# A two-layer hybrid decoder trunk on one core: attention in visits of two token tiles, retention's queries and keys in one product, weight places and delays set anew

## The chip, the core and the metric

The kernel runs on one NeuronCore of a Trainium2 chip. A core has a matrix engine (TensorE, PE in the profile, with its weight loads as PEld), a vector engine (VectorE, DVE), a scalar engine (ScalarE, ACT), GpSimd (POOL) and a SyncE queue (SP) that issues most DMAs. Each engine works through its own list of instructions in order and waits on semaphores for the others. The metric is the device time of one execution in microseconds, lower is better. Before the change three runs took 1002.16, 1005.88 and 1008.02 us, the median being 1005.88.

## What is computed

Two layers (DEPTH = 2) over 1024 tokens of width 1024, all in 32-bit floats. In each layer one projection feeds three groups of heads whose outputs are gated, joined and projected back:

```python
h = rms_norm(x, pre_gain) * (1.0 + scale) + shift
proj = h @ w_in
(aq, ak, av, ag, rq, rk, rv, rg, gq, gk, gv, gg, ga) = jnp.split(proj, IN_SPLITS, axis=-1)
a_out = sliding_window_attention(aq, ak, av, sinks) * jax.nn.silu(ag)
r = retention(rq, rk, rv.reshape(B, S, RET_HEADS, RET_DV))
r_out = rms_norm(r).reshape(B, S, RET_W) * jax.nn.silu(rg)
g_out = rms_norm(g, gla_norm_gain).reshape(B, S, GLA_W) * jax.nn.silu(gg)
y = jnp.concatenate([a_out, r_out, g_out], axis=-1) @ w_out
return x + gate * rms_norm(y, post_gain)
```

`scale`, `shift` and `gate` come from a product with `w_mod`; `g` is gated linear attention (GLA); `aq`, `ak`, `rq` and `rk` are rotated by position first. Attention has 8 query heads on 2 key heads, a window of 128 tokens and a learned sink per head in the softmax. Retention has 4 heads of 64 with a fixed decay per head and runs in chunks of 128.

## The kernel before

**Tiles.** The tokens make 8 tiles of 128 (t = 0 to 7), two to a pair (p), four to a half (hf). The input weights are loaded in units of 256 columns: gg, rg (gates), rq, rk, rv (retention), gqk, gv (GLA), kv, aq0, aq1 (attention), ag0, ag1 (its gates), and o0 to o3 of the output projection. For accuracy each operand of the large products is held as a rounded part and a remainder; a product sums three of the four combinations (`PASSES`) over 8 blocks of depth, so 24 matmuls (`accum`). `project` makes one tile by one unit, so matmuls of 256 columns; `project_T` makes 128 weight columns by four tiles, matmuls of 512 columns, its two halves named by `both`. All matmuls are recorded on one line, that of the helper `mult` (L173), and transposes on that of `transp` (L188); products go into `mm` banks of PSUM (3), everything else into `aux` banks (5).

**Stages of a layer.** Gates (`do_gates`), retention (the loop over p with rq, rk, rv), GLA's products (`do_gqk`, `do_gv`) with keys and values of attention (`do_kv`), rotated queries (`attn_rot`), attention with the ag products, output projection. Retention, GLA and attention cores are generators (`ret_core`, `gla_core`, `attn_q`), called jobs, cut into steps by `yield`.

**What sets the order.** TensorE's order is the order in which the program is written. While it is built, `clk` adds up the assumed TensorE time; every `yield` names a delay from the table `L`, and `pump`, called between and inside products, runs each job step that is due. So the table decides how many products lie between, say, a tile's scores and its transposes. `flag` and `await_flag` make steps wait for one another on the same clock. In a product with 512 columns `pump` is called after every 4 matmuls, with 256 after every 7. The other engines' lists are ordered by a scheduler from the same program.

**Attention before.** `attn_run` visits one tile of one half and one key head g: `attn_q` makes the scores of 4 heads in two `aux` banks (12 matmuls, 64 rows of the array each), moves them to SBUF (`smx`, line 157 for the previous block's copy on ScalarE, line 936 for the masked one on VectorE), takes the maximum (938), four exponentials (941), the reciprocal (944) and the scaling on POOL (945). After `aq3` it transposes the four heads into one bank; ScalarE copies, POOL masks (`affine_select`). After `aq4` it multiplies with the values `va` and their differences `vd`, and stores the result to `aoS`.

**Weights.** A unit arrives in four parts of 256 KB through staging buffers (`st`, 5, shared with the `w_mod` stream), each issued on SP; ScalarE or VectorE writes the rounded part (157, 159), VectorE or POOL the remainder (546). `PLACE` says into which of the seven places of SBUF a unit goes, and so which earlier unit must be done with. `load` is called when that one is.

Of the kernel before, what the change touches and what calls it, by code (L numbers as in the profile page):

```python
# [10 lines left out]
F32 = mybir.dt.float32  # L11
# [36 lines left out]
TURNED = ("gqk", "aq0", "aq1", "ag0", "ag1")  # L48
TOKEN_AT, PLAIN_AT, TURNED_AT, OUT_AT, BLOCK_AT = 48, 0, 48, 0, 64
PLAIN = 2  # L50
SW = dict(W00=6, T1=3, W11=4, W10=5, T2=2, T3=0, T4=1)
TOK = ((1, 2, 3, 4), (3, 4, 0, 1))
PLACE = []
for _t, _w in zip(TOK, (0, 2)):
    PLACE.append(dict(gg=_w, rg=5, rq=6, rk=_w, rv=5, gqk=6, gv=_w, kv=5, aq0=6, aq1=_w, ag0=5, ag1=_w,
                      o0=_t[0], o1=_t[1], o2=5, o3=6))
# [37 lines left out]
def trunk(ctx: ExitStack, tc: tile.TileContext, ins, cst, out):  # L94
# [53 lines left out]
    def both(x, y):  # L148

        return bass.AP(x.tensor, x.offset, [x.ap[0], (y.offset - x.offset, 2), (1, 256)])  # L150
# [489 lines left out]

    def project_T(pm, l, hf, w, c):
# [259 lines left out]
    def attn_run(l):  # L901

        for hf in range(2):
            for g in range(2):
                for t in range(4 * hf, 4 * hf + 4):
                    yield (lat("aq7" if hf else "aq1", l), ("q", l, hf, g))
                    yield (0.0, ("kT", l, t))
                    job(attn_q(l, t, g, kv[(hf, g)]))

    def attn_q(l, t, g, q):  # L910

        sm = gp.tile([P, 4, 129], F32, tag="smx", name=nm("smx"), bufs=SMB)
        V.tensor_copy(sm[:, :, 128], sink8[:, l, 4 * g:4 * g + 4])
        if t == 0:
            G.memset(sm[:, :, 0:128], -1e30)
        else:
            vd = gp.tile([P, P], F32, tag="vd", name=nm("vd"), bufs=3)
            G.tensor_tensor(vd, kv["v"][t], kv["v"][t - 1], ALU.subtract)
        pss = [aux(), aux()]
        n = P if t == 0 else 2 * P  # L920
        cols = slice((t + 1) * P - n, (t + 1) * P)
        for j in range(2):
            qc = slice(P * (t % 4), P * (t % 4) + P)
            for i, (a, b) in enumerate(PASSES):
                for r in range(2):
                    rr = slice(64 * r, 64 * r + 64)
                    mult(pss[r][:, j * n:(j + 1) * n], q[rr, a, j, qc], kv["kT"][b][rr, cols],
                         i == 0, i == 2, n / 4600.0)
        if t % 4 == 3:
            flag(("s", l, t // 4, g))  # L930
        for r in range(2):
            pv = pss[r][:, 0:2 * n].rearrange("p (j c n) -> p j c n", j=2, n=P)
            sv = sm[:, r:4:2, 0:128]
# [794 lines left out]
```

## Time and profile before

| | |
|---|---|
| three runs | 1002.16, 1005.88, 1008.02 us |
| profiled execution | 1000.26 us |
| its span, first to last instruction | 998.5 us |
| mean granted TensorE clock | 0.987 |
| TensorE idle over 1 us, by its waits | 29.2 us in fifteen groups, the largest 7.4 us |
| DMA moved | 148.76 MB, 149 GB/s on average |

The lines of the profile name engine, line, operation and tiles as out<-in; times are us from the start of the span. A timeline row gives start, length, engine, instruction, count and, in brackets, the idle time before it with what released it. Because matmuls are pipelined and their ends are modelled, a row's length overlaps the next one; what a group costs TensorE is the distance from its start to the next start.

### The profile page before, as it was taken

The numbers are of one execution on the slowest core, as the hardware profiler recorded it, in microseconds if no ns is written. First come the engines' busy times: TensorE is split into PE (matmuls) and PEld (weight loads), VectorE is DVE, ScalarE is ACT, GpSimd is POOL, SyncE is SP. The second block draws the span as 40 slices with busy tenths as digits, with TensorE's granted clock in tenths as the row PEclk, the third lists the DMA queues.
The fourth block names the chain that finished last, engine by engine and source line by source line (L and its number), as shares of the span: only waits on it lengthen the run. The fifth ranks groups of instructions, "written<-read, shape, count | busy, mean of one in ns | idle before, by whom it ended". The sixth has DMA issues, their size and how long they took to land.

```text
span 998.5 us, 19629 instructions
## 1 busy us (share of the span) xinstructions
PE 961.3 (96%) x7133; PEld 825.5 (83%) x7133; DVE 690.5 (69%) x1698; ACT 409.6 (41%) x1152; POOL 236.0 (24%) x275
## 2 busy tenths in 40 slices
PE   5798999999999999999999999999999999999896
PEld 2598999888998777778889999998899877777675
DVE  3779856857767778664588285685666577676886
ACT  2476411324332556542356242123333267664231
POOL 2210101232330234330113010113332034555000
PEclk8899999999999999999999999999999999999998
DMA  9832613523326255668646151343132433487883
GB/s 315 296 114 79 186 48 88 161 89 101 110 81 188 79 154 155 203 192 259 228 150 203 49 175 38 106 136 116 41 107 85 127 90 123 131 247 242 262 268 136
DMA packets 129968, 148.76 MB, mean 149 GB/s; under 512 B 14112, under 2 KB 94284, under 8 KB 129872
## 3 DMA queue, kind: packets, MB, share of 16 engines
q1 hardware_dynamic: 124176, 137.96, 45.2%
q10 hardware_dynamic: 5696, 9.56, 2.5%
q8 instruction: 56, 0.92, 0.4%
q14 instruction: 40, 0.33, 0.1%
HBM read 109.20 MB, written 36.18 MB: 146 GB/s over the span
## 4 chain that ended last, share of the span: by engine, by line
PE 75%; DVE 10%; DMA 7%; ACT 3%; issue 3%; POOL 2%; SPq 1%; ACTq 0%; POOLq 0%; DVEq 0%
PE mm L173 56%; PE aux L173 14%; PE aux L188 4%; DMA st<-in_w_in_dram 2%; POOL sm L650 2%; DMA t<-mixF 1%; DMA xk<-in_x_dram 1%; DMA t<-in_x_dram 1%; DMA aoS<-t 1%; DMA a<-mixS 1%; DVE arena L546 1%; DVE arena L723 1%; ACT t L666 1%; DVE t L715 1%; SPq L162 1%
## 5 line engine op out<-in xcount | busy, mean ns | idle before, releaser
L173 PE MATMUL mm<-arena 128*128 128x256 f32 (+2 forms) x1824 | 299.5, 318 | 4.2 <-DVE t L1008 2.7
L173 PE MATMUL mm<-arena,arena 128*128 128x256 f32 (+2 forms) x1824 | 297.4, 316 | 0.3 <-DVE t L1008 0.3
L173 PEld LDWEIGHTS mm<-arena 128*128 128x128 f32 x1824 | 255.3, 191 | 28.4 <-issue 3.3
L173 PEld LDWEIGHTS mm<-arena,arena 128*128 128x128 f32 x1824 | 252.5, 188 | 23.9 <-issue 4.3
L650 POOL TENSOR_TENSOR sm<-sm,mhalf 128x1 f32<-128x1 f32 (+1 forms) x64 | 55.9, 874 | 347.3 <-DVE sm L649 334.9
L173 PE MATMUL mm<-arena,mx 128*128 128x512 f32 (+1 forms) x564 | 128.2, 383 | 1.4 <-ACT kept L1355 1.4
L173 PEld LDWEIGHTS mm<-arena,mx 128*128 128x128 f32 x564 | 101.6, 188 | 22.9 <-ACT kept L1355 1.8
L157 ACT ACTIVATE t<-aux 128x256 f32<-128x256 f32 (+2 forms) x124 | 55.9, 468 | 73.7 <-PE aux L188 62.5
L157 ACT ACTIVATE arena<-st 128x512 fp32r<-128x512 f32 x94 | 55.9, 626 | 51.2 <-PE mm L173 19.0
L546 POOL TENSOR_TENSOR arena<-st,arena 128x512 fp32r<-128x512 f32 x31 | 43.3, 1401 | 133.2 <-ACT arena L157 96.7
L945 POOL TENSOR_TENSOR smx<-smx,sm 128x512 f32<-128x512 f32 x32 | 36.4, 1138 | 124.2 <-DVE sm L944 114.2
L546 DVE TENSOR_TENSOR arena<-st,arena 128x512 fp32r<-128x512 f32 x77 | 59.1, 787 | 5.9 <-ACT arena L157 3.7
L941 ACT ACTIVATE smx<-smx,sm 128x129 f32<-128x129 f32 x128 | 49.9, 392 | 27.8 <-DVE sm L938 27.8
L188 PE MATMUL aux<-c_ident,t 128*128 128x128 f32 (+1 forms) x292 | 48.6, 284 | 7.8 <-DVE t L681 7.4
L375 DVE SCALAR_TENSOR_TENSOR acc<-st,c_act,acc 128x512 f32<-128x512 f32 x60 | 45.4, 757 | 14.1 <-DMA st<-in_w_mod_dram 13.6
L188 PEld LDWEIGHTS aux<-c_ident,t 128*128 128x128 f32 (+1 forms) x292 | 35.2, 145 | 15.0 <-DVE t L681 9.4
L989 ACT ACTIVATE t<-aux 128x256 f32<-128x256 f32 x32 | 12.3, 384 | 75.7 <-PE aux L173 72.2
L173 PEld LDWEIGHTS aux<-t,mx 32*128 32x128 f32 (+1 forms) x896 | 39.5, 187 | 3.8 <-issue 2.0
L713 ACT ACTIVATE t<-aux,mod,mod 128x128 f32<-128x128 f32 x68 | 25.7, 459 | 37.0 <-DVE t L1262 19.4
L173 PE MATMUL aux<-t,mx 32*128 32x32 f32 (+1 forms) x896 | 40.6, 272 | 0.0
L936 DVE COPY_PREDICATED smx<-c_curmask,aux 128x256 f32<-128x256 int32 x64 | 25.5, 447 | 16.0 <-ACT smx L157 13.0
L1262 DVE SCALAR_TENSOR_TENSOR t<-t,sm,t 128x512 f32<-128x512 f32 x32 | 24.0, 780 | 17.8 <-DMA t<-in_x_dram 11.5
(223 smaller groups left out, 1382.9 us busy)
## 6 DMA issues: line engine op xcount, KB each, us to landing
st<-in_w_in_dram SPq DMA_DIRECT2D x96, 256.0 KB, 3.1
st<-in_w_mod_dram SPq DMA_DIRECT2D x64, 256.0 KB, 2.8
st<-in_w_out_dram SPq DMA_DIRECT2D x52, 256.0 KB, 3.7
mx<-mixS SPq DMA_DIRECT2D x20, 512.0 KB, 4.9
mixS<-t SPq DMA_DIRECT2D x72, 128.0 KB, 3.1
wm<-in_w_mod_dram SPq DMA_DIRECT2D x12, 512.0 KB, 6.6
t<-in_x_dram SPq DMA_DIRECT2D x24, 256.0 KB, 4.9
t<-tabS SPq DMA_DIRECT2D x16, 256.0 KB, 3.8
```

What stands on the lines that cost most here:

```text
L157: A.activation(dst, src, AF.Copy)
L173: T.matmul(dst, lhsT, rhs, start=start, stop=stop)
L188: T.transpose(dst, src, idn)
L375: V.scalar_tensor_tensor(acc, wt, c_act[:, k:k + 1], acc, ALU.mult, ALU.add)
L546: e.tensor_tensor(lo, st, f(hi), ALU.subtract)
L650: G.tensor_tensor(r, r, mhalf[:, :w], ALU.pow)
L713: A.activation(hf[:, ks], at[kt], AF.Identity, scale=gain, bias=shift)
L936: V.copy_predicated(sv, curmask.unsqueeze(1).to_broadcast((P, 2, P)), pv[:, :, n // P - 1, :])
L941: A.activation(sm[:, h, :], sm[:, h, :], AF.Exp, bias=mx[:, h:h + 1], accum_out=sums[:, h:h + 1])
L945: eng("pn").tensor_tensor(sm[:, :, 0:128], sm[:, :, 0:128], rs.unsqueeze(2).to_broadcast((P, 4, P)), ALU.mult)
L989: A.activation(sq, po, AF.Square)
L1262: V.scalar_tensor_tensor(xt[j], yg[j], r, xt[j], ALU.mult, ALU.add)
```

## The change

Five things change together.

1. `attn_q` becomes `attn_two`: a visit takes the tiles t and t + 1. Scores of both (four `aux` banks), then softmax of both, one delay, transposes of both (two banks), one delay, value products of both into the two halves of one bank, one copy of 512 columns, two stores. There are 16 visits in place of 32. `smx` has 4 buffers in place of 3, `vd` 4 in place of 3, the small tiles 13 in place of 11.
2. In retention `project2` multiplies a tile with rq and rk in one product of 512 columns; `both` joins the two units, for which they stand in the same arena. For each pair the values (rv) come first, then the joint product of either tile. `rv` is loaded after gg, `rk` after rg.
3. `PLACE` and `SW` are dealt anew, `rq` and `rk` start at a different offset of their place, and o3, ag1 and W00 are loaded at exchanged points.
4. The table `L` is set anew: `aq1` 6.0 to 12.0, `aq3` 10.21 to 14.0, `rc1` 0.8 to 8.5, `ld2` 1.2 to 0.8, and some forty more.
5. Two paddings of SBUF and a DMA scratch size (4096 to 1024) differ.

```diff
-TURNED = ("gqk", "aq0", "aq1", "ag0", "ag1")
+TURNED = ("gqk", "aq0", "aq1", "ag0", "ag1", "rq", "rk")
...
-    PLACE.append(dict(gg=_w, rg=5, rq=6, rk=_w, rv=5, gqk=6, gv=_w, kv=5, aq0=6, aq1=_w, ag0=5, ag1=_w,
-                      o0=_t[0], o1=_t[1], o2=5, o3=6))
+    PLACE.append(dict(gg=_w, rg=5, rq=6, rk=5, rv=_w, gqk=_w, gv=5, kv=6, aq0=_w, aq1=5, ag0=6, ag1=_w,
+                      o0=_t[0], o1=_t[1], o2=6, o3=5))
...
+    def project2(l, t, u, v):
+        w0, w1 = used(l, u), used(l, v)
+        await_flag(("hT", l, t))
+        c = slice((t % 2) * P, (t % 2) * P + P)
+        h = hT[(l, t // 2)]
+        pm = mm()
+        accum(pm.rearrange("p (s n) -> p s n", s=2), lambda a, k: h[:, a, k, c],
+              lambda b, k: both(w0[:, b, k, 0:256], w1[:, b, k, 0:256]))
+        return pm
...
-    def attn_q(l, t, g, q):
+    def attn_two(l, ts, g, q):
...
+        for t in ts:
+            pss[t] = [aux(), aux()]
...
+                for i, (a, b) in enumerate(PASSES):
+                    for r in range(2):
+                        rr = slice(64 * r, 64 * r + 64)
+                        mult(pss[t][r][:, j * n:(j + 1) * n], q[rr, a, j, qc], kv["kT"][b][rr, cols],
+                             i == 0, i == 2, n / 4600.0)
...
+        yield lat("aq3", l)
+
+        mv = {}
+        for t in ts:
+            pp = aux()
+            for h in range(4):
+                transp(pp[:, h * P:(h + 1) * P], sms[t][:, h, 0:128], ident)
+            pf = t2()
+            copy("pf0", pf, pp)
...
         yield lat("aq4", l)
         po = aux()
...
-        ao = t1()
-        copy("aoc", ao, po[:, 0:256])
...
+        ao = t2()
+        copy("aoc", ao, po)
+        for i, t in enumerate(ts):
+            dma("sao", aoS[t, :, 2 * g:2 * g + 2, :], ao[:, 256 * i:256 * i + 256].rearrange("p (k q) -> p k q", k=2))
+            flag(("ao", l, t, g), lat("aq5", l))
...
-            for name in ("rq", "rk", "rv"):
...
+            for t in (2 * p, 2 * p + 1):
+                pm = project2(l, t, "rq", "rk")
+                q, k = (ret_rot(t, pm[:, 256 * i:256 * i + 256], d) for i, d in enumerate((qdec, kdec)))
+                job(ret_core(l, t, q, k, rr[t]))
+                pump()
+            if last:
+                load(l, "gv")
+                load(l, "kv")
...
-B2, B1, BS, BST, MMB, SMB = 10, 8, 11, 5, 3, 3
+B2, B1, BS, BST, MMB, SMB = 10, 8, 13, 5, 3, 4
```

How this moves instructions is seen in the built order of each engine. First TensorE in layer 0's attention, before the change: one visit's value products, a stretch of products, the next visit's transposes, and the first rows of another visit's scores (ten more rows alternate between the same two banks).

```order
L173 MATMUL aux_4965<-t_847_4837,va_3446 64x256 x2
L173 MATMUL aux_4965<-t_848_4839,vd_4672 64x256 x2
L173 MATMUL mm_4923<-arena_322 128x512 x20
L188 MATMUL aux_5004<-c_ident,smx_4860 128x128 x4
L173 MATMUL aux_5021<-kT_3225,mx_4358 128x256
L173 MATMUL aux_5022<-kT_3225,mx_4358 128x256
```

The same place of TensorE's order after the change (`smx` is a tile's softmax, `va` and `vd` its values, `mm` the product stream, `kT` and `mx` keys and queries).

```order
L174 MATMUL mm_4618<-arena_72 128x512 x12
L189 MATMUL aux_4720<-c_ident,smx_4471 128x128 x4
L189 MATMUL aux_4729<-c_ident,smx_4475 128x128 x4
L174 MATMUL mm_4618<-arena_72 128x512 x8
L174 MATMUL mm_4752<-arena_322 128x512 x24
L174 MATMUL mm_4789<-arena_322 128x512 x4
L174 MATMUL aux_4794<-t_853_4725,va_3249 64x256 x2
L174 MATMUL aux_4794<-t_854_4727,vd_4473 64x256 x2
L174 MATMUL aux_4794<-t_856_4734,va_3411 64x256 x2
L174 MATMUL aux_4794<-t_857_4736,vd_4477 64x256 x2
L174 MATMUL aux_4819<-kT_3030,mx_4183 128x256
L174 MATMUL aux_4820<-kT_3030,mx_4183 128x256
```

Small matmuls now come in groups twice as long with longer stretches of products between: 36 products lie between a pair's transposes and its value products.

A little later in TensorE's order after the change, the last two rows of that visit's 24 score matmuls and what follows them.

```order
L174 MATMUL aux_4833<-kT_3031,mx_4183 128x256
L174 MATMUL aux_4834<-kT_3031,mx_4183 128x256
L189 MATMUL aux_4878<-c_ident,smx_4641 128x128 x4
L189 MATMUL aux_4887<-c_ident,smx_4645 128x128 x4
L174 MATMUL mm_4789<-arena_322 128x512 x20
L174 MATMUL mm_4935<-arena_322,arena_72 128x512 x16
L174 MATMUL aux_4974<-t_886_4883,va_3558 64x256 x2
```

Here the transposes of the previous visit follow the scores with no product between; their second bank, the fifth `aux` bank after the first of these scores, is that score bank again.

Then ScalarE at the end of layer 0's retention, before the change. The rows from `st` are conversions of the last three parts of kv that ScalarE takes, `t_419` is the copy of a tile's turned queries and keys for which `ret_core` waits, `t_410` a tile's values, `t_415` a finished output.

```order
L157 ACTIVATE arena_322<-st_2483 128x512
L157 ACTIVATE arena_322<-st_2495 128x512
L157 ACTIVATE t_410_2428<-mm_2367 128x256
L157 ACTIVATE arena_322<-st_2524 128x512
L157 ACTIVATE t_415_2443<-aux_2440 128x256
L157 ACTIVATE t_419_2458<-aux_2453 128x512
```

The same place on ScalarE after the change; `t_400` is now the copy that `ret_core` waits for.

```order
L158 ACTIVATE arena_322<-st_2262 128x512
L1015 ACTIVATE t_383_2166<-aux_2151 128x256
L158 ACTIVATE arena_322<-st_2303 128x512
L158 ACTIVATE t_389_2186<-aux_2183 128x256
L158 ACTIVATE arena_322<-st_2349 128x512
L158 ACTIVATE arena_322<-st_2367 128x512
L158 ACTIVATE t_400_2229<-aux_2224 128x512
```

`st_2262` is the last part of gv; the two last parts of kv stand directly ahead of the copy, where before one part and a finished output did.

## What was predicted

> **What bounds the kernel now.** I read the page's busy line first, then the chain that ended last, then TensorE's waits, then the windows.
>
> ```profile
> PE 961.3 (96%) x7133; PEld 825.5 (83%) x7133; DVE 690.5 (69%) x1698; ACT 409.6 (41%) x1152; POOL 236.0 (24%) x275
> PE 75%; DVE 10%; DMA 7%; ACT 3%; issue 3%; POOL 2%; SPq 1%; ACTq 0%; POOLq 0%; DVEq 0%
> ...
> PE aux L188 <- DVE t L681: 7.4, 4, 3.7
> PE aux L188 <- DVE posr L416: 6.0, 1, 6.0
> PE aux L173 <- ACT t L157: 4.6, 2, 3.3
> PE mm L173 <- DVE t L1008: 3.0, 3, 2.1
> ...
> 175.00:200.00 25.00, 22.43 (x183) 21.27 (x181) 19.74 (x55) 7.80 (x16) 5.54 (x5) 1.00 0.58 165
> 200.00:225.00 25.00, 24.32 (x142) 21.14 (x143) 14.58 (x38) 6.23 (x15) 8.04 (x10) 0.93 0.29 89
> 375.00:400.00 25.00, 25.00 (x158) 18.61 (x158) 21.22 (x39) 16.32 (x50) 11.43 (x12) 1.00 0.52 159
> 850.00:875.00 25.00, 25.00 (x161) 17.82 (x160) 17.41 (x34) 16.24 (x54) 13.15 (x14) 1.00 0.42 130
> ```
>
> The first two lines: TensorE is busy 96% of the span and carries 75% of the chain. The next four head the list of TensorE's waits (total, times, longest); its fifteen lines sum to 29.2 us of 998.5. The windows (TensorE, weight loads, VectorE, ScalarE, POOL, then granted clock) show no idle TensorE in either attention stage (25.00 of 25.00). So almost everywhere the time is what TensorE's own instruction order costs, and an edit counts by what it does to that order, plus any wait it creates.
>
> **Retention's queries and keys as one product.** Rows of the groups by form, and two pieces of the chain:
>
> ```profile
> L173 PE MATMUL mm<-arena 128*128 128x256 f32 x1152 | 151.2, 285 | 2.7 <-DVE t L1008 2.7
> L173 PE MATMUL mm<-arena,arena 128*128 128x256 f32 x1152 | 150.2, 284 | 0.0
> L173 PE MATMUL mm<-arena,arena 128*128 128x512 f32 x480 | 122.1, 402 | 0.0
> L173 PE MATMUL mm<-arena 128*128 128x512 f32 x480 | 120.6, 399 | 0.0
> ...
> 475.62 10.91 PE mm L173 x48
> 634.93 5.66 PE mm L173 x48
> ```
>
> The means of 285 and 402 ns are latencies of pipelined matmuls; what one costs is busy time over count. The edit turns 768 matmuls of 256 columns (8 tiles, 2 weights, 24 each, 2 layers) into 384 of 512. Undisturbed, 48 of 512 take 10.91 us (227 ns each) and 48 of 256 take 5.66 us (118 ns): 768 x 0.118 - 384 x 0.227 = 3.4 us. The groups give the same: 301.4/2304 = 131 and 242.7/960 = 253 ns, 3.4 us. **Term A: -3.4 us.**
>
> The Trainium skill (TensorE: Matmul & The Clock Gate, Back-to-back issue gap) puts the warm gap at N/2.4 plus 2.5 ns, so a merged pair would save only 2.5 ns, 1.0 us in all, and the sum would shrink by 2.4 us; it also names 131 ns as the sustained spacing at 512 columns. The trace disagrees with both: 227 ns, and 9 ns saved for a pair.
>
> VectorE's rotations are the same in number. One bank now waits for two of them, but the bank is next needed three products later, as before. Cost: nothing.
>
> **Attention by two tiles.** A stretch of TensorE's timeline (start, length, columns as on the page). An instruction group's real cost is the distance to the next start:
>
> ```profile
> 385.01 0.60 PE L173 MATMUL aux<-t,vd 128*64 128x256 f32 x4
> 385.54 0.98 PE L173 MATMUL aux<-kT,mx 64*128 64x256 f32 x12
> 386.45 3.93 PE L173 MATMUL mm<-arena 128*128 128x512 f32 x16
> 390.21 0.60 PE L188 MATMUL aux<-c_ident,smx 128*128 128x128 f32 x4
> 390.57 1.18 PE L173 MATMUL mm<-arena 128*128 128x512 f32 x4
> 391.67 0.98 PE L173 MATMUL aux<-kT,mx 64*128 64x256 f32 x12
> 392.58 0.65 PE L173 MATMUL aux<-t,va 128*64 128x256 f32 x4
> 393.07 0.60 PE L173 MATMUL aux<-t,vd 128*64 128x256 f32 x4
> 393.60 4.84 PE L173 MATMUL mm<-arena 128*128 128x512 f32 x20
> 398.27 0.60 PE L188 MATMUL aux<-c_ident,smx 128*128 128x128 f32 x4
> ```
>
> Sixteen products between 386.45 and 390.21 take 3.76 us, where 16 x 0.227 is 3.64: each return from the small matmuls costs 0.12 us. Four products (390.57 to 391.67) take 1.10 for 0.91: 0.19 us. Over the whole built order TensorE leaves the product stream 208 times before and 177 times now (attention 63 to 36). **Term B: 31 x 0.155 = -4.8 us**, between 3.7 and 5.9.
>
> Inside a visit, scores cost 0.91 us, transposes 0.36, the value products 0.49 + 0.53. Two tiles together lose one seam in each of the three groups. The trace has no double group, so I bound it: nothing below; above, 0.2 for scores, 0.3 for transposes and 0.2 for values. I take 0.15 (as a return), 0.10 and 0.05. **Term C: 16 visits x 0.30 = -4.8 us**, between 0 and 11.
>
> The Trainium skill (TensorEngine Tiling (Array Packing), Key Properties) says that changing the tiling mode drains the array, a change of tile does not. The returns above agree in kind. By it the score and value seams, which keep their mode, would each save the larger 0.19 us, and the sum would be 16 x (0.38 - 0.20) = 2.9 us larger.
>
> ScalarE's 32 output copies become 16 of twice the width, and as many DMAs are issued; neither engine sets the pace there (ScalarE 16.3 of 25).
>
> **What must cover the longer visit.** One tile's way from scores to transposes:
>
> ```profile
> 362.24 0.98 PE L173 MATMUL aux<-kT,mx 64*128 64x256 f32 x12
> 363.25 0.66 ACT L157 ACTIVATE smx<-aux 128x256 f32<-128x256 f32 x2 [1.18 <-PE aux L173]
> 365.43 0.78 DVE L936 COPY_PREDICATED smx<-c_curmask,aux 128x256 f32<-128x256 int32 x2
> 366.25 0.69 DVE L938 TENSOR_REDUCE sm<-smx 128x4 f32<-128x516 f32 x1
> 366.97 0.40 ACT L941 ACTIVATE smx<-smx,sm 128x129 f32<-128x129 f32 x1 [2.30 <-DVE sm L938]
> 368.65 0.18 DVE L944 RECIPROCAL sm<-sm 128x4 f32<-128x4 f32 x1 [1.72 <-ACT smx L941]
> 368.91 1.46 POOL L945 TENSOR_TENSOR smx<-smx,sm 128x512 f32<-128x512 f32 x1 [3.95 <-DVE sm L944]
> ```
>
> Scores end about 363.2 and the weights stand ready at 370.4: 7.2 us. A second tile in series adds 0.66 + 0.78 + 0.69 + 1.7 (four exponentials) + 0.2 + 1.46 = 5.5 us, 12.7 in all. The new order puts about 52 products (11.8 us), a pair's transposes, a value group and the next scores (3.9 us) between a visit's scores and its transposes: 15.7 us. The cover holds with 3 us to spare. If it fails, TensorE waits the shortfall at each visit, with the product stream queued behind it, and VectorE and ScalarE wait for that.
>
> The tight place is banks. A visit takes four score banks, two for transposes and one for values, from five; so the second transposes bank is the visit's own first score bank. Usually 4 to 12 products lie between; at one place in each layer none do, and TensorE waits there for ScalarE's copy and VectorE's masked copy. **Term D: +1 us** for the two (0 to 8 with the others).
>
> **The handover from retention to the next stage.**
>
> ```profile
> st<-in_w_in_dram SPq DMA_DIRECT2D x96, 256.0 KB, 3.1
> ...
> 193.91 0.48 SPq L162 DMA_DIRECT2D st<-in_w_in_dram  x1
> 199.24 0.63 ACT L157 ACTIVATE arena<-st 128x512 fp32r<-128x512 f32 x1 [2.85 <-DMA st<-in_w_in_dram]
> 199.78 0.85 ACT L157 ACTIVATE t<-aux 128x256 fp32r<-128x256 f32 x2
> 200.68 1.20 PE L173 MATMUL aux<-t 64*128 64x128 f32 x8 [3.26 <-ACT t L157]
> ```
>
> ScalarE works in order: a weight conversion waited for a part that landed 5.3 us after its issue, the copy of turned queries and keys stood behind it, and TensorE waited 3.26 us. After the change the last two kv parts still stand ahead of that copy, and they now need staging buffers that gv frees only once the keys' place is free. Two conversions (0.63 each), issue (0.5), landing (3.1 by the first row to 5.3), conversion and copy (0.6 + 0.6) make 6.1 to 8.3 us. TensorE has sixteen products and four transposes (3.6 + 0.4) in that time, which leaves a wait of 2 to 4.3 us, much like today's. **Term E: 0**, between -3 and +2. The other delays move work within stages that show no TensorE wait, or DMAs ahead of use; I count nothing for them.
>
> **The sum.** -3.4 - 4.8 - 4.8 + 1 = -12.0 us. The profiled execution took 1000.26 us and would take 988.3; the median of the runs shown lies 5.6 us above it, at 1005.88, so I forecast **993.9 us** for runs like those. By the bounds of A to E it ends between 984 and 1003.
>
> **Rivals.** (1) *The waits go too*: if the new SyncE and ScalarE order clears the handover in layer 0 (3.3 us idle and the 0.93 clock, 1.7 us in the window) and most of its smaller twin in layer 1, another 5 to 7 us fall: 988. For it: the last kv part is no longer queued behind a store. Against: the same conversions stand ahead of the same copy. (2) *The saving is waited away*: VectorE is busy 21.22 of 25 us in attention, and its masked copies came 2.2 us after ScalarE's (363.25, 365.43) behind modulation work. If each visit overruns its cover by 0.5 us, 8 us come back: 1002. Against: 3 us of spare cover. (3) *Slower, by banks*: if masked copies come that late at each visit, TensorE stands before the second transposes bank for up to 2.2 us, less the products between; at 1.5 us for each of 16 visits that is 24 us, 1018. It decides against the change from 17/16 = 1.1 us a visit. Against: at most visits 4 to 12 products (0.9 to 2.7 us) lie between.
>
> **How the numbers follow.** Forecast 0.60, (1) 0.15, (2) 0.17, (3) 0.08. The forecast and (1) lie on the fast side; 0.5% (about what a measurement here can tell from no change) is 1000.9, which a little of the forecast's upper end passes and about a fifth of (2) stays below. Faster 0.74, same 0.18, slower 0.08. The range 984 to 1004 takes in the forecast, nearly all of (1), most of (2), and leaves out about 0.15.
>
> **What would show it.** A: in the groups by form, 1,536 matmuls of 256 columns in place of 2,304 and 1,344 of 512 in place of 960, at 118 and 227 ns. B and C: score groups of 24 in about 1.65 us and attention stages some 4.5 us shorter each. D and E: TensorE's waits stay near 29 us, a row of 2 to 5 us before L174 at the handover. A wait for smx from VectorE or ScalarE in attention, repeated at many visits, would make the prediction wrong, as would a waits total above 40 us.

## The result and the profile after

The change made the kernel faster, but by less than half of what was forecast. Over 11 runs of each the median went from 1005.12 to 1001.01 us; the ratio is **0.9948, with a 95% interval of 0.9928 to 0.9968**, about 5 us where 12 were forecast. The profiled execution of the changed kernel took 1001.01 us (span 999.0), against a forecast of 988.3 on that scale.

The busy line of the changed kernel's page, and TensorE's waits (total, times, longest), to be read beside those of before:

```profile
PE 956.4 (96%) x6749; PEld 814.3 (82%) x6749; DVE 692.0 (69%) x1698; ACT 406.1 (41%) x1137; POOL 232.0 (23%) x275
...
PE aux L189 <- DVE t L692: 7.5, 4, 2.8
PE aux L189 <- DMA wm<-in_w_mod_dram: 5.5, 1, 5.5
PE mm L174 <- ACT kept L1381: 4.8, 1, 4.8
PE aux L189 <- DVE smx L955: 4.8, 3, 2.6
PE aux L189 <- DVE t L855: 2.2, 1, 2.2
PE mm L174 <- DVE t L1385: 2.2, 3, 1.1
...
PE mm L174 <- DVE t L1034: 1.2, 1, 1.2
```

Two old waits shrank: the handover's L173 behind ScalarE from 4.6 us to 1.1 (most of it now behind VectorE), and the gates' L1008, which is line 1034 after the change, from 3.0 to 1.2. New are one for masked copies in attention (L955, 4.8) and one for turned keys (L855, 2.2). The wait for a bank of the last stage (`kept`) is 4.8 us. The first profile of before has 1.4 there, but a second one, taken later, has 4.0, so this wait is not new:

```profile
PE mm L173 <- ACT kept L1355: 1.4, 1, 1.4
...
PE mm L173 <- ACT kept L1355: 4.0, 1, 4.0
```

The second half of the story is in the clock. Windows laid over the stretches in which TensorE was granted half its clock (columns as in the prediction; TensorE's busy time, then the clock and the DMA share, follow the length), of before:

```profile
84.70:88.11 3.41, 3.41 (x18) 3.41 (x18) 3.41 (x9) 1.83 (x5) 0.00 (x0) 0.50 0.11 38
200.75:204.16 3.41, 3.41 (x14) 2.70 (x15) 0.76 (x2) 0.00 (x0) 0.46 (x1) 0.50 0.81 238
...
sum 26.36, PE 17.05 PEld 14.47 DVE 17.30 ACT 8.24 POOL 6.24; mean PE 3.41 PEld 2.89 DVE 3.46 ACT 1.65 POOL 1.25
```

and of the changed kernel:

```profile
223.26:226.67 3.41, 3.41 (x18) 3.41 (x17) 3.15 (x9) 0.73 (x4) 1.66 (x4) 0.50 0.37 108
301.76:305.18 3.42, 3.42 (x11) 2.74 (x10) 3.32 (x11) 0.39 (x1) 0.00 (x0) 0.50 0.66 189
533.87:537.28 3.41, 3.41 (x17) 3.41 (x16) 2.49 (x9) 3.41 (x11) 0.55 (x1) 0.50 0.18 64
834.24:837.65 3.41, 3.41 (x12) 2.92 (x11) 2.01 (x5) 1.45 (x7) 0.00 (x0) 0.50 0.73 215
933.23:940.06 6.83, 5.48 (x13) 4.32 (x14) 5.37 (x13) 2.45 (x6) 0.56 (x1) 0.50 0.70 215
...
sum 38.41, PE 29.76 PEld 24.41 DVE 25.27 ACT 13.92 POOL 8.95; mean PE 3.72 PEld 3.05 DVE 3.16 ACT 1.74 POOL 1.12
```

Half of the busy time in such windows is lost: 17.05/2 = 8.5 us before, 29.76/2 = 14.9 us after. That splits the span into three parts, which are used for every run below. **Idle** is the span less TensorE's busy time, **half clock** is this loss, and **work** is the rest.

| profile | span | idle | half clock | work |
|---|---|---|---|---|
| before | 998.5 | 37.2 | 8.5 | 952.8 |
| before, once more (below) | 1006.7 | 39.9 | 14.4 | 952.4 |
| changed | 999.0 | 42.6 | 14.9 | 941.5 |

The work fell by 11.3 us, near the 13.0 of the prediction's terms A to C. Waits took 5.4 back and half clock 6.4. So the spans of the two profiles differ by only 0.5 us. The first profile of before was a lucky one: over 95 further runs of it the mean span is 1003.2 us at a mean clock of 0.9845 (15.6 us of span times missing clock), and the 11 runs of the changed kernel have 998.0 at 0.9826 (17.3 us). Over the runs the difference is therefore 5.2 us: 6.9 in work and waits, less 1.7 in clock.

### The profile page after: what moved, and what is told of

Read it like the earlier page. It is cut to its first block, busy times and chain, and to the rows that moved or that the text cites. A ratio compares the mean times of both kernels' runs of the same rounds, so it can differ in the third digit from the quotient of the medians.

```text
span 999.0 us, 18797 instructions
## 1 busy us (share of the span) xinstructions
PE 956.4 (96%) x6749; PEld 814.3 (82%) x6749; DVE 692.0 (69%) x1698; ACT 406.1 (41%) x1137; POOL 232.0 (23%) x275
## 5 line engine op out<-in xcount | busy, mean ns | idle before, releaser
L174 PE MATMUL mm<-arena 128*128 128x256 f32 (+2 forms) x1632 | 295.3, 335 | 2.9 <-ACT arena L730 1.8
L174 PEld LDWEIGHTS mm<-arena 128*128 128x128 f32 x1632 | 246.0, 191 | 31.7 <-ACT arena L730 2.0
L174 PEld LDWEIGHTS mm<-arena,arena 128*128 128x128 f32 x1632 | 244.3, 190 | 29.5 <-DVE t L1034 1.4
L174 PE MATMUL mm<-arena,mx 128*128 128x512 f32 (+1 forms) x564 | 130.8, 389 | 6.2 <-ACT kept L1381 4.8
L158 ACT ACTIVATE t<-aux 128x512 f32<-128x512 f32 (+2 forms) x108 | 51.8, 504 | 66.0 <-PE aux L189 45.1
L966 POOL TENSOR_TENSOR smx<-smx,sm 128x512 f32<-128x512 f32 x32 | 34.0, 1064 | 132.0 <-DVE sm L965 131.0
L174 PEld LDWEIGHTS aux<-t,mx 32*128 32x128 f32 (+1 forms) x896 | 40.4, 187 | 4.0 <-issue 2.2
L1020 DVE TENSOR_TENSOR t<-aux,sm 128x256 f32<-128x256 f32 x32 | 13.6, 425 | 27.9 <-POOL sm L661 27.9
```

The source lines that it names most:

```text
L158: A.activation(dst, src, AF.Copy)
L174: T.matmul(dst, lhsT, rhs, start=start, stop=stop)
L966: eng("pn").tensor_tensor(sm[:, :, 0:128], sm[:, :, 0:128], rs.unsqueeze(2).to_broadcast((P, 4, P)), ALU.mult)
L1020: V.tensor_tensor(h4(g1), h4(po), r.unsqueeze(2).to_broadcast((P, 4, 64)), ALU.mult)
```

## The experiments

The ratios are to the kernel before, on the same chip; a microsecond is 0.001. The last three columns are from the profile of each.

| run | median us | ratio (95%) | idle | half | work |
|---|---|---|---|---|---|
| changed kernel | 1001.0 | 0.9948 (0.9928 to 0.9968) | 42.6 | 14.9 | 941.5 |
| no_merge | 1006.4 | 1.0020 (1.000 to 1.004) | 45.2 | 16.1 | 946.0 |
| one_tile | 997.1 | 0.9928 (0.9901 to 0.9956) | 36.1 | 10.4 | 952.5 |
| t2_bank | 998.1 | 0.9929 (0.9904 to 0.9954) | 40.0 | 9.1 | 943.1 |
| aq3_late | 1000.5 | 0.9962 (0.9943 to 0.9980) | 43.2 | 11.3 | 944.4 |
| one_t2 | 999.6 | 0.9946 (0.9926 to 0.9965) | 34.5 | 7.7 | 952.2 |
| free_gate_after | 997.8 | 0.9936 (0.9922 to 0.9951) | 45.6 | 8.3 | 942.1 |
| free_gate_before | 1005.6 | 1.0009 (0.9992 to 1.0026) | 38.9 | 9.9 | 952.8 |
| light_after | 995.4 | 0.9901 (0.9873 to 0.9928) | 41.0 | 7.1 | 943.9 |
| light_before | 997.2 | 0.9925 (0.9898 to 0.9951) | 32.7 | 8.9 | 952.5 |
| b2_11 | 1000.0 | 0.9953 (0.9927 to 0.9978) | 43.8 | 11.8 | 942.7 |
| keep_warm | 1000.6 | 0.9946 (0.9925 to 0.9966) | 42.6 | 8.6 | 945.2 |
| delays_back | 1009.3 | 1.0025 (1.0004 to 1.0047) | 51.7 | 21.1 | 941.1 |
| merge_alone | 1076.9 | 1.0718 (1.0684 to 1.0752) | 90.5 | 32.8 | 956.1 |
| mmb2 | 1022.7 | 1.0182 (1.0154 to 1.0210) | 63.2 | 17.5 | 945.0 |
| pp_mm | 997.7 | 0.9935 (0.9909 to 0.9960) | 43.7 | 14.9 | 941.1 |
| best | 995.7 | 0.9905 (0.9879 to 0.9931) | 40.4 | 13.7 | 942.6 |

### The kernel before, once more

No edit.

> The kernel before, unchanged, profiled once more: the first profile (1000.26 us) lay 5 us below the median of its runs. If what differs between executions is idle TensorE and stretches of half clock, this profile shows the same TensorE work (span less idle less half the time at half clock, 948 us) and more of the other two, and its time lies near 1005. If the first profile was typical and the runs merely add something outside the span, the span is again 998 to 999 us with 37 us idle and a clock of 0.987.

The work was 952.4 us (952.8 in the first profile), idle 39.9 and half clock 14.4: what differs between executions is waits and clock, and the last column repeats to half a microsecond here. It does not always repeat so well: the changed kernel and the edits of it that leave TensorE's matmuls as they are (t2_bank, free_gate_after, light_after, b2_11, pp_mm) lie between 941.1 and 943.9. (The expectation takes off half of all time at half clock, idle time included, and so has 948; by that count the two are 948.2 and 948.1.)

### Each half of the change undone

```diff
-                pm = project2(l, t, "rq", "rk")
+                    pm = mm()
+                    project(pm[:, 0:256], l, t, w)
```

> The changed kernel with retention's queries and keys as two products of 256 columns again, everything else as changed. Theory (the work fell as computed and was given back in waits and half clock elsewhere, mostly after the last attention visit): 768 x 0.118 less 384 x 0.227 = 3.4 us of TensorE work come back, and the time rises by 3 to 4 us against the changed kernel, so it lies some 1 to 2 us under the kernel before. Rival (the merge saved nothing that reaches the end, since what follows the stages waits for weights anyway): no change against the changed kernel, within 1 us.

```diff
-                    job(attn_two(l, (t, t + 1), g, kv[(hf, g)]))
+                    job(attn_q(l, t, g, kv[(hf, g)]))
```

This run also has `attn_q` and attention's five delays as in the kernel before.

> The changed kernel with attention by one tile per visit again and the five delays of attention set as before, everything else as changed. Theory (seams and returns saved 8 to 9 us of TensorE work, of which the waits for masked copies in attention, 4.8 us, and one or two stretches of half clock, 1.7 us each, took most back): TensorE work rises by 8 to 10 us, its waits in attention vanish, and the time rises by 0 to 4 us. Rival (double visits saved little): the work rises by under 4 us and the time falls by 2 to 5 us.

Without the merge the work rises by 4.5 us and the time by about 7, since waits and half clock grew as well. The merge does reach the end. With visits of one tile the work rises by 11.0 us, and yet the time falls to 0.9928: idle time is 6.5 us less and half clock 4.5 less, and the waits for masked copies are gone. Of these 11 us, 4.7 lie in the last stage and the rest ahead of it. **The two-tile visit saves what was predicted on TensorE and gives all of it back.** The intervals of this run and of the changed kernel overlap, so it is not shown that one tile is better; it is shown that two are no gain here.

The work by kind of matmul (distance from each start to the next, idle and half clock taken out), in us:

```
                         before  one_tile  no_merge  changed
products of 256 columns   282.9     189.9     285.0    189.8
products of 512 columns   231.4     322.0     226.4    316.7
attention's small ones     73.1      73.0      67.7     67.5
all others                365.0     367.3     366.5    367.2
```

### The waits in attention

> The changed kernel with two delays longer: aq3 from 14.0 to 16.0 and aq3@1 from 12.5 to 15.0, so that at least 8 products lie between a visit's scores and the transposes of the visit before (0 to 8 at most places in the changed kernel). Theory (the 4.8 us of waits for masked copies and one stretch of half clock in attention come from a bank that is wanted too early): these waits go, TensorE leaves the product stream ten times more (188 for 178, 1.5 us), and the time falls by 3 to 5 us against the changed kernel. Rival (the wait is VectorE being late as such, and what is gained before the last visit is lost at the stage behind it): the waits shrink, and the time stays within 1.5 us.

Here only `aq3` and `aq3@1` differ. The waits shrank (layer 0's attention has no idle left, layer 1's has 2.4 us, 1.02 of it for a masked copy), and the work rose by 2.9 us with ten more returns, hardly more than the work scatters without a cause. The time is 1.4 us above the changed kernel, within the intervals: a longer cover gained nothing.

```diff
-B2, B1, BS, BST, MMB, SMB = 10, 8, 13, 5, 3, 4
+B2, B1, BS, BST, MMB, SMB = 10, 8, 13, 5, 2, 4
```

> The changed kernel with two banks for products and six for the rest, in place of three and five. Theory (attention's 4.8 us of waits arise because the second bank for transposes is a score bank of the visit just made): with six banks it is not, these waits and their stretch of half clock go without more returns to the product stream, and the time falls by 3 to 6 us. Rival (products need the third bank: with two, each product waits until VectorE or ScalarE has read the one before the last): waits of products appear in the stages with 256 columns, and the time rises by 2 us or more.

TensorE's waits with six banks for attention and two for products, the masked copy's last:

```profile
PE mm L174 <- DVE t L1034: 15.8, 7, 3.9
PE mm L174 <- DVE t L1625: 11.4, 5, 9.0
...
PE aux L189 <- DVE smx L955: 1.1, 1, 1.1
```

Both were right about their own part. The masked copies cost 1.1 us in place of 4.8, so the fifth bank is what TensorE waits for; and products need their third bank: 27 us in the first two rows, where the changed kernel has 1.2.

```diff
-            pp = aux()
+            pp = aux() if t == ts[0] else mm()
```

> The changed kernel with the transposes of a visit's second tile put into a product bank in place of the fifth of the other banks; the order of TensorE stays. Theory (the attention waits are for that one bank, as the run with six banks suggests, 4.8 us to 1.1 us): the waits for masked copies fall below 1 us, no return to the product stream is added, and the time falls by 2 to 6 us against the changed kernel (ratio to before 0.989 to 0.993). Rival (VectorE is late, and what waits there only moves to the next scores or products): idle TensorE in the attention stages stays at 4 us or more and the ratio at 0.994 to 0.996.

```profile
832.48 1.12 PE L189 MATMUL aux<-c_ident,smx 128*128 128x128 f32 x4 [2.81 <-DVE smx L955]
833.39 1.06 PE L189 MATMUL mm<-c_ident,smx 128*128 128x128 f32 x4
...
904.50 2.07 PE L174 MATMUL mm<-arena,mx 128*128 128x512 f32 x4 [2.60 <-ACT t L158]
```

In layer 0 the waits went (the stage fell from 125.9 to 124.2 us). In layer 1 the first transposes wait 2.81 us for the same late masked copy, as they did in the changed kernel (2.59): the value products that stand ahead of them there take the fifth bank, so it is the first tile's transposes that come to a score bank, and the edit moves only the second tile's. The product bank that was borrowed makes a product wait 2.60 us for ScalarE. The time is 1 us under the changed kernel, which the intervals don't tell apart.

### The last stage

```diff
-            pm = mm()
+            pm = aux()
             prod(pm, cur.s2, "T2")
```

> The changed kernel with the product T2 of the last output stage in one of the five other banks, so that it no longer waits for ScalarE's copy out of the bank of W00; the instruction lists of all engines stay the same. Theory (the 4.84 us of idle TensorE there and the 6.8 us of half clock that begin in it are lost time that the change made, and its operands stand ready from about 930.5 us): the wait shrinks to about 1 us, the half clock goes, and the time falls by 4 to 6 us. Rival (this stage is bound by the stream of output weights and the stores and loads of the gated outputs, not by the bank): the wait moves to one of the next three products, and the time falls by less than 1.5 us.

> Attention by one tile with the delays of before, the rest as changed, and the product T2 of the last output stage in another bank. Theory (with one tile per visit the last gates are done earlier, so that the bank of W00 is no longer what TensorE waits for there): no more than 1 us under the run with one tile alone, 996 to 998. Rival (the bank costs both alike): 2 us under it, 994 to 995.

The wait of 4.84 us became four of 1.4 to 2.1 (before a product `ma`, T2, T4 and the next W00), and the stage from W00 to the end took 99.3 us in place of 99.8. The 2 us of the ratio are not told apart from none. The same edit beside one-tile visits gave nothing either (0.9946 after 0.9928). The bank was not the limit.

```diff
-                yield (0.0, ("ao", l, t, g))
+                yield (0.0, ("ao", l, t, 0 if l and hf else g))
-            dma("lao", ao.rearrange("p (t q) -> p t q", t=4), rows(aoS, hf, k))
+            dma("lao", ao.rearrange("p (t q) -> p t q", t=4), rows(aoS, hf, kk if l and hf else k))
```

> The changed kernel, but in layer 1 the gates of the second half's key head 1 multiply with the stored attention outputs of key head 0, so they wait for nothing from the last two visits (these are computed and stored, but not read). Theory (what the visits save is given back behind the last value products: output copy on ScalarE, store, load and gate on VectorE stand in a row ahead of the last stage's sums, 21.8 us from the value products to the store of the gated part, where the kernel before takes 15.9 and 19.0): the stretch from the first product W00 to the end shrinks from 99.8 to 94 us or less, and the time falls by 5 to 7 us against the changed kernel. Rival (the last stage is bound by the stream of weights or by its loads of x): it shrinks by less than 2 us.

> The same edit in the kernel before (gates of key head 1 in layer 1's second half read the outputs of key head 0). Theory: there the row is shorter (from the first product W00 to the end 93.3 and 95.6 us), so the time falls by only 0 to 3 us; the difference between the two kernels with this edit is near 10 us. Rival (the row costs both alike): it falls by as much as in the changed kernel, and the difference stays near 5 us.

The store of the last gated part came 13 us sooner after the value products (8.8 us in place of 21.8), and the stage took 99.7 us. The time fell by 1.2 us, within the intervals, and the kernel before with the same edit stayed where it was (1.0009). My theory, that this row of steps bounds the stage, fell.

```diff
-            s3, x = sw_load(k, 0, 1), sw_load(k, 1, 1)
-            sw_diff(s3, 1, k, x, s3)
-            s2, s4 = sw_load(k, 0, 0), sw_load(k, 1, 0)
-            eng("sd").tensor_tensor(s2, s3, s2, ALU.add)
-            sw_split("T2", k, s2, "t2")
+            s3, s4 = sw_load(k, 0, 1), sw_load(k, 1, 0)
+            sw_split("T2", k, s3, "t2")
...
-            sw_diff(s4, 1, k, s4, s2)
```

> The changed kernel with a lighter stream of output weights in the last stage: of the 16 parts for T2, T3 and T4 only 8 are loaded, and their 12 sums on VectorE are left out. Theory (the saving ahead of it is given back at this stream: TensorE comes to the product W00 6 us earlier, but the parts land and are summed on VectorE at the same absolute time, and the sums that release the banks of the products stand behind them): the stretch from W00 to the end shrinks from 99.8 to 95 us or less, and the time falls by 4 to 8 us against the changed kernel. Rival (the stage is bound by the order of TensorE and its loads of x, as in the kernel before): it shrinks by less than 2 us.

> The same lighter stream in the kernel before. Theory: there the stream is nearly hidden by the work on TensorE (from W00 to the end 93.3 and 95.6 us), so the time falls by only 0 to 3 us, and the changed kernel is ahead of it by 8 to 11 us with this edit in both. Rival (the stream costs both alike): the difference stays near 5 us.

The stage shrank from 99.8 to 93.9 us in the changed kernel, but also from 93.3 (95.6 in the second profile) to 88.9 in the kernel before; the ratios are 0.9901 and 0.9925. So the stream of T2 to T4 through VectorE costs both kernels 4 to 7 us, and the theory that it alone eats the saving fell as well: with it halved, the stage of the changed kernel is still 5.0 us longer than that of the kernel before. TensorE's waits in it are then none before and 3.2 us after, behind loads and sums. Where the stream does cost the changed kernel more is told under "The last stage" in the next section.

> The changed kernel with eleven buffers of 512 columns in SBUF in place of ten. A visit of two tiles takes five of them where two visits of one took four and two small ones; ahead of the last stage ScalarE stands 4.2 us before a copy into such a buffer, with the first conversions of T2 and T3 queued behind it. Theory (this wait is what holds the stream back): the time falls by 2 to 5 us against the changed kernel. Rival (the conversions wait for something else at the same time): no change, within 1.5 us.

One number differs (B2 from 10 to 11). The time did not change. The copy that waited for a buffer came 4.5 us sooner (905.15 us in place of 909.68), but the conversions behind it then waited up to 3.6 us for VectorE's sums of the output weights, and from 914 us on ScalarE's times are within 0.2 us of those before the edit. The buffer was a wait, but not the one that sets the pace.

### The clock

```diff
             a22 = cur.a22()
+            if p == PLAIN // 2:
+                prod(aux(), cur.a[1], "W10")
```

> The changed kernel with the product W10 made a second time, into a spare bank that nothing reads, where TensorE is idle for 4.84 us in the last stage (12 matmuls, 2.7 us). Theory (an idle stretch of TensorE is followed by 3.4 or 6.8 us at half the granted clock, and that is part of what the change lost): the half clock near 933 us goes, and the time falls by 1 to 3 us against the changed kernel. Rival (the clock falls at fixed places or at random, whatever TensorE does): no half clock less, the time the same within 1 us.

In the profile the half clock at 932 us lasted 3.4 us in place of 6.8. Over 11 runs the span times the missing clock fell from 17.3 to 13.5 us, and the rest of the span rose by 4.0. Idle time and half clock are coupled, as the theory has it, but work made up to fill the gap costs as much as the clock gives: the time is the same.

### The table of delays

> The changed kernel with the table of delays of before, but for attention's (aq1, aq3, aq4, aq5, aq7) and retention's (rc1 to rc4), which stay changed. Theory (of the new waits, the 2.2 us before the turned keys at 300 us and the 1.9 us before the first transposes of layer 1 at 533 us come from delays set shorter, kv1, kv2 and pre1 among them, and each is followed by 3.4 us of half clock): both go, and the time falls by 3 to 6 us against the changed kernel (ratio to before 0.989 to 0.992). Rival (VectorE is late there behind weights that still arrive, whatever the delays): they stay, and the time is within 1.5 us of the changed kernel.

> Retention merged, places, paddings and buffers as changed, but attention by one tile and the whole table of delays as before. Theory (the rest of the table costs TensorE some 4 us of work: the run with one tile kept the work of the kernel before, 952, although the merge saves 4.5): the work is 948 us, and the ratio to before 0.992 to 0.997. Rival (the merge saves its 4.5 us only next to visits of two tiles, or the places and buffers cost as much): the work is 952 again.

Both edits are entries of `L` alone (the second with `attn_q` as in one_tile). The first took the wait at 300 us away and halved the one at 533 us, but the kernel became some 8 us slower (1.0025). Idle time rose by 9 us in all: up to retention's first core from 16.2 to 21.6, at layer 1's handover 3.17 in one piece, and half clock by 6 with it. The second shows why the table had to move:

```profile
PE aux L189 <- DVE t L1182: 51.7, 32, 4.6
```

Those are 32 waits of 1.6 us, two at each tile of either layer, before retention's transposes: with `rc1` at 0.8 us they come before VectorE has rotated both halves of the joint product. So the merge can't be had without the longer delay; the prediction priced both kernels' tables at nothing. With that many waits the work can't be read to a few us (each restart is counted in it), so whether the rest of the table costs TensorE work stays open.

### Three edits together

pp_mm, t2_bank, and `kv1` and `kv2` at 3.1 and 2.11:

> The same, with T2 of the last stage in another bank as well, and kv1 and kv2 of layer 0 as before (3.1 and 2.11 us), whose wait at 300 us went when the whole table was set back. Theory: attention gives 2 to 6 us, T2 about 2, the keys 2 to 4 with their half clock, so the ratio to before is 0.983 to 0.990. Rival (each of them only moves the wait to the last stage, whose loads and sums stand still): 0.991 to 0.994.

0.9905 (0.9879 to 0.9931), between the two expectations: about 4 us faster than the changed kernel, with intervals that just touch, and clearly faster than the kernel before. Keys and layer 0's attention wait no more; layer 1 and the last stage kept theirs, and in this profile the handover of layer 0 waits 2.3 us.

## Why the prediction missed

**In short.** The work fell nearly as forecast. What failed is the rest of the sum: +1 for new waits (D), and nothing for the other delays and for the last stage. Between the first profiles, counting idle time with the half clock behind it, D cost 6.5 us where 1 was allowed, the other delays 9.2 and the last stage 5.7 where nothing was; the handover gave back 5.2 and the gates 3.5. That makes 12.7 us, near the 11.8 by which idle and half clock grew. Single profiles scatter by some us in these terms, so this order of size is less certain than the terms themselves.

**The scale.** The first profile of before lay 5 us below its runs, about half of it in clock and half in waits. The forecast kept that distance for the changed kernel, whose own profile lies at its median; so the two profiles alone hide a gain that the runs show. The range was added up too narrow: the bounds given for A to E reach from 982 to 1009 us, not from 984 to 1003. The measured 1001.01 lies inside both.

**A, the merge (-3.4): right.** The undone merge costs 4.5 us of work. Next to one-tile visits the products fell by 282.9 + 231.4 - 189.9 - 322.0 = 2.4 us, but all other matmuls took 2.3 us more there, so that in one_tile the whole work did not fall.

**B and C, the visits (-4.8 and -4.8): right.** Between one_tile and the changed kernel attention's small matmuls lost 5.5 us and the products 5.4 to 28 fewer returns (0.19 each, the upper end). The three kinds of A to C fell by 13.4 us in all between the kernels, where the terms sum to 13.0. The parts of C show in the timeline of the changed kernel:

```profile
381.45 1.69 PE L174 MATMUL aux<-kT,mx 64*128 64x256 f32 x24
383.07 3.02 PE L174 MATMUL mm<-arena 128*128 128x512 f32 x12
385.93 1.03 PE L189 MATMUL aux<-c_ident,smx 128*128 128x128 f32 x8
386.72 8.45 PE L174 MATMUL mm<-arena 128*128 128x512 f32 x36
...
407.81 0.65 PE L174 MATMUL aux<-t,va 128*64 128x256 f32 x4
408.29 0.60 PE L174 MATMUL aux<-t,vd 128*64 128x256 f32 x4
408.73 0.60 PE L174 MATMUL aux<-t,va 128*64 128x256 f32 x4
409.16 0.60 PE L174 MATMUL aux<-t,vd 128*64 128x256 f32 x4
409.69 1.70 PE L174 MATMUL aux<-kT,mx 64*128 64x256 f32 x24
```

Scores of two tiles take 1.62 us (0.20 saved, 0.15 taken), transposes 0.79 (nothing saved, 0.10 taken), values 1.88 (0.16 saved, 0.05 taken). The total of C came out nearly right, with another split. What the terms left out is the last row of the table of kinds: 2.2 us more in all other matmuls, whose cause was not looked for.

**D, the banks (+1): right in kind, wrong in size and place.** The waits are 4.8 us at three visits, and one brought a stretch of half clock (1.7): 6.5 us. The mechanism was rival 3's, at three visits in place of sixteen. The step counted spare products and took VectorE to be on time; it was not (TensorE's rows first, then VectorE's, `smx` from L955 being the masked copy):

```profile
369.07 0.60 PE L189 MATMUL aux<-c_ident,smx 128*128 128x128 f32 x4
371.27 0.63 PE L189 MATMUL aux<-c_ident,smx 128*128 128x128 f32 x4 [1.60 <-DVE smx L955]
...
396.98 1.70 PE L174 MATMUL aux<-kT,mx 64*128 64x256 f32 x24
398.60 1.09 PE L189 MATMUL aux<-c_ident,smx 128*128 128x128 f32 x8
...
833.79 1.59 PE L189 MATMUL aux<-c_ident,smx 128*128 128x128 f32 x8 [2.59 <-DVE smx L955]
...
370.01 0.75 DVE L376 SCALAR_TENSOR_TENSOR acc<-st,c_act,acc 128x512 f32<-128x512 f32 x1 [2.43 <-DMA st<-in_w_mod_dram]
370.68 0.78 DVE L955 COPY_PREDICATED smx<-c_curmask,aux 128x256 f32<-128x256 int32 x2
...
831.58 0.94 DVE L580 TENSOR_TENSOR arena<-st,arena 128x512 fp32r<-128x512 f32 x1
832.44 0.94 DVE L587 TENSOR_TENSOR st<-st,st 128x512 f32<-128x512 f32 x1
833.30 0.77 DVE L955 COPY_PREDICATED smx<-c_curmask,aux 128x256 f32<-128x256 int32 x2
```

In layer 0 the masked copy that frees the bank stands in VectorE's list behind modulation work, which waits 2.43 us for its weights. In layer 1, where the longest wait is, VectorE is not waiting but busy with other work, last with output weights (831.58 and 832.44). Rival 2 named the modulation work, and rival 3 put the late copy at this bank. The sum kept its 1 us for the two places without spare products, and at these (398.60, and 858.67 in layer 1) TensorE did not wait at all. The three waits have 4, 4 and 12 products between scores and transposes (from 368.04, 828.13 and 870.55). What decides is when VectorE comes to the masked copy, not how many products stand between.

**E, the handover (0): it improved, as in rival 1.** In layer 0 the wait fell from 3.26 to 0.92 us, and the 3.4 us of half clock behind it are gone:

```profile
193.15 0.78 PE L174 MATMUL aux<-t 64*128 64x128 f32 x8 [0.92 <-DVE t L1008]
```

That is 4 us to the good in this profile, and of layer 1's 1.3 only 0.2 is left. The wait at this place is not steady: the other profiles of kernels with the changed table and the joint product have from nothing up to 2.3 us here, the longest (best) with half clock behind it. Why the last part of kv came in time was not tested.

**"I count nothing for the other delays": wrong.** The keys (2.2 us, half clock behind it) and the first transposes of layer 1 (1.9, likewise) wait where nothing waited before, and a stretch of half clock stands at 223 us with no wait at all: 4.1 us of waits and 5.1 of half clock. Both waits are there with one-tile visits too (2.3 and 1.9 in one_tile), so they do not come from the visits.

**The last stage: not priced.** The sum let every saving ahead of it reach the end. TensorE came to W00 at 899.2 us where it had come at 905.2, and in the second profile of before at 911.1. The stage then took 99.8 us where it had taken 93.3 and 95.6 (windows of before, of before once more, and of the changed kernel):

```profile
905.20:998.50 93.30, 81.48 (x371) 66.16 (x369) 68.54 (x119) 28.66 (x65) 15.35 (x16) 0.97 0.71 225
...
911.10:1006.70 95.60, 83.68 (x371) 67.81 (x369) 69.61 (x123) 29.05 (x65) 15.45 (x16) 0.95 0.71 226
...
899.16:999.00 99.84, 85.02 (x377) 68.43 (x375) 72.81 (x125) 28.75 (x64) 18.15 (x18) 0.94 0.70 216
```

About 1 us of it is work that moved in, the rest waits and half clock. TensorE's waits in the changed kernel:

```profile
926.73 3.02 PE L174 MATMUL mm<-arena,ma 128*128 128x512 f32 x12 [0.78 <-DVE t L1385]
934.58 1.65 PE L174 MATMUL mm<-arena,mx 128*128 128x512 f32 x3 [4.84 <-ACT kept L1381]
```

All of the loss lies ahead of VectorE's first sum of an output, which here is the row of before and then that of the changed kernel:

```profile
922.15 0.68 DVE L1359 TENSOR_TENSOR t<-aux,kept 128x512 f32<-128x512 f32 x1
...
922.81 0.68 DVE L1385 TENSOR_TENSOR t<-aux,kept 128x512 f32<-128x512 f32 x1
```

Before the change this sum stands 17.0 and 19.3 us behind W00 in the two profiles, after it 23.7; from there to the end all three take 76.1 to 76.4 us. Up to that sum VectorE adds up the parts of the output weights. In the runs with the lighter stream the sum stands 12.8 us (before) and 13.7 us (changed) behind W00, so most of the difference ahead of it belongs to this stream: an earlier TensorE mostly waits for it. The lighter changed kernel then takes 80.2 us from the sum to the end, the lighter kernel before 76.1, and the cause of that is open. Rival 2 had the outcome (the saving waited away, 1002) with a chance of 0.17, at the wrong place.

## What to carry to other kernels

Where one engine is busy 96% of the time, shortening its list moves it closer to all the others: price each place where its slack was small, not only the list. Split spans into work, idle and half clock and compare several executions: here the work repeats to within 3 us, and to half a microsecond in the two profiles of before, while one profile's waits and clock move the span by 8. An edit that only takes the longest wait away may not pay, since the next late engine can be about as late: here two such edits gave 1 to 2 us each, within their error, and about 4 with a third.

## What the hardware showed

Half clock follows idle TensorE, and sooner than I had taken for granted. In 19 profiles, from 60 us on, a stretch of half clock of 3.41 us or a multiple began in or within 3.5 us behind 24 of 24 idle stretches of 3 us or more, 34 of 57 between 1.8 and 3 us, and 13 of 108 between 0.8 and 1.8 us. A wait of 2 us thus costs up to 3.7. The Trainium skill (TensorE: Matmul & The Clock Gate, Part 1: The HAM clock gate) describes a free-running window of 3.4 us and puts the drop behind at least one idle window. The traces agree with the length and with the free run: in each profile all starts of half clock lie whole numbers of 3.413 us apart. They do not agree that a whole window must be idle. Cut into such windows, the 19 profiles from 60 us on have 65 windows at full clock with 1.8 us or more of idle TensorE, and 60 of them were followed by half clock; of the other 5018 it was 12. So a wait is dear when more than half of one window falls into it, and where the windows lie differs from one execution to the next. Of two windows of the changed kernel (TensorE's busy time behind the length), the first, with 2.18 us idle, was followed by half clock; the second holds 1.1 us of the 1.60 us wait that ends at 371.27, whose rest fell into the next window, and was not:

```profile
298.35:301.76 3.41, 1.23 (x7) 0.93 (x7) 3.41 (x10) 1.01 (x4) 1.28 (x1) 1.00 0.43 110
...
367.38:370.80 3.42, 2.29 (x21) 1.69 (x18) 0.99 (x3) 1.48 (x4) 0.00 (x0) 1.00 0.73 218
```

Nine more stretches, eight of them at 220 to 237 us, came without such a wait, next to GLA's matmuls of 32 rows and 32 columns:

```profile
220.44 2.34 PE L174 MATMUL aux<-t,mx 32*128 32x32 f32 x47
...
223.23 3.33 PE L174 MATMUL mm<-arena,arena 128*128 128x256 f32 x14
```

Fourteen products then take 3.13 us to the next start, 224 ns each where 118 are usual. Small matmuls seem to count as little activity: of the windows with less than 1 us of idle TensorE and more than 0.5 us of these matmuls, all 11 in which the two make 2.3 us or more were followed by half clock, and none of 291 in which they make 1.0 to 2.2 us. That is read off the traces; no run was made to test it.
